# A two-layer encoder trunk on one core: a sixteenth place for expert weights, rows from 128 on stored behind the pair's rows, idle products on the matrix engine, and gathers by expert pair

## The chip, the core and the metric

One core of a Trainium2 chip runs the whole program. Five engines work side by side: PE (matrix products), DVE and ACT (elementwise work and reductions; ACT also has function tables that must be loaded), POOL, and SP, which here only issues transfers. Each runs its own instructions in order and waits on semaphores for the others. Weights come from the chip's memory through 16 DMA engines. The metric is the device time in microseconds (us) of one execution; less is better.

## The reference, cut to what matters

256 tokens of width 1024 go through two layers. Each layer has a mixer (two linear recurrences, attention over all tokens, gates) and a feed-forward part. In the first layer this part is dense (width 2816); in the second it is eight experts of width 3584, of which a router picks two for each token:

```python
def moe_swiglu(h, router_w, router_b, w_gate, w_up, w_down):
    t = h.reshape(B * S, D)
    logits = (t @ router_w).astype(jnp.float32) + router_b.astype(jnp.float32)
    top_vals, top_idx = lax.top_k(logits, TOP_K)
    top_w = jax.nn.softmax(top_vals, axis=-1)
    combine = jnp.sum(jax.nn.one_hot(top_idx, N_EXPERTS) * top_w[..., None], axis=1)
    for e in range(N_EXPERTS):
        y = swiglu(t, w_gate[e], w_up[e], w_down[e])
        out = out + combine[:, e:e + 1] * y
...
h = modulate(x, sh1, sc1); x = x + g1 * hybrid_mixer(h, ...)
h = modulate(x, sh2, sc2); x = x + g2 * ff
return rms_norm(x, final_gain)
```

Everything is float32, and the expert weights are 352 MB of the 516 MB that are read.

## The kernel before, in words

**Dense stages.** Mixer, dense feed-forward and second mixer are one list of units (34, 33 and 34 of them). A unit is a weight block of 128 x 2048 floats (1 MB). ACT rounds it to a high part, DVE or POOL makes the low part, and PE multiplies high and low parts with those of the activations, 48 products of 256 columns in a unit (L397). `Run.go` writes the units one after the other, and `run.at(u, pe, ev)` hangs other work on a unit; that written order is the order on each engine.

Three places of these stages matter here. `Norm.scale` (L344 to L351) stands between two stages: the sums of squares (L316, products with one column), the root on ACT and DVE (`root`), a diagonal matrix `dg` on DVE, and one product `rb` that spreads the row factors over all partitions; DVE then makes `h` (L375), ACT `hh` (L377), DVE `hl` (L364), and the first unit starts. `heads` (L676 on) does attention two heads at a time: scores, softmax on ACT, DVE and POOL, and `turn_pe` (L701), which transposes the probabilities on PE into banks `prT`; the first two heads of a layer have nothing before them that PE could do meanwhile. In `moe`, the router picks (DVE), five small products count each expert's tokens (`posp`, L1098 to L1102), and DVE makes positions from them.

**Experts.** The eight experts are handled in four pairs. Each pair has 84 weight blocks of 1 MB, two to a unit: 42 units in the order of the table `TOGETHER`, which alternates the pair's experts A and B. The blocks of all pairs run through a ring of `R["size"]` places, 15 here, in a fixed order: before unit i, SP may issue the blocks up to 2i + 15 of the pair (`fetch_moe`), as far as the places they go to have been read. The tokens of an expert are gathered into `xs` by products with a one-hot matrix: `pick` makes it on DVE, `gather` (L1126) does 8 products of 128 columns for each half of the width, and ACT or DVE scales the result. Expert 0 is gathered before the first branch, expert 1 inside pair 0, and those of the next pair inside a pair, at units 13, 14 and 19, 20. Rows of an expert from 128 on are gathered at the start of its own pair into another buffer, `xbig`, which holds the place of `xT`.

What a pair does depends on how many tokens its two experts got: a `Switch` (L1485) on a register jumps to one of five written-out ways or to a general one. In the execution profiled here, pairs 0 and 3 have at most 64 rows for each expert, pair 1 has 96 and 64, pair 2 has 160 and 32. After the last pair all ways join again, and the final norm and the output (L1490 to L1500) follow.

Of the kernel before, what the change touches and what calls it, by code (L numbers as in the profile page):

```python
# [38 lines left out]
def trunk(tc, a, out, dbg=None):  # L39
# [38 lines left out]
    def pd(name, shape):  # L78
        return psp.tile(shape, F32, name=name, tag="d", bufs=4)

# [217 lines left out]
    class Norm:  # L298
# [162 lines left out]
    def mixer(l, nrm, run, U):  # L461
# [210 lines left out]
        def heads(h0, u):  # L672
# [175 lines left out]
    def ffn(nrm, run, U):  # L848
# [85 lines left out]
        def pre():  # L934
            nrm.scale(pd)
            M["hh"], M["hl"] = nrm.split(0, 3, 4)
# [107 lines left out]
    def moe(nrm):  # L1044
# [9 lines left out]
        R["ring"].append(buf("big2", [128, 2048], F32, "ring2"))  # L1054
        assert len(R["ring"]) == R["size"]
# [40 lines left out]

        pp = pd("posp", [128, 3, 8])
# [14 lines left out]
        xs = [big("xs", F32, (128, 2, ND, 128)) for _ in range(2)]  # L1112
        xbig = act.tile([128, 2, ND, 128], F32, name="xbig", tag="xT", bufs=1)
# [6 lines left out]
        def pick(e, second=False):  # L1120

            oh = buf("t1k", [128, 2, 128], name="oh")
            for t in range(2):
                V.tensor_scalar(oh[:, t, :], iota, (pos2 if second else pos)[:, t, e:e + 1], None, op0=OP.is_equal)
            return oh

        def gather(oh, x, q):

            p = pm("gat", [128, 4, 128])
            for j in range(4):  # L1130
                k = 4 * q + j
                for t in range(2):
                    PE.matmul(p[:, j, :], th[:, t, k * 128:(k + 1) * 128], oh[:, t, :], start=(t == 0), stop=(t == 1))  # L1133

            def ev():
                for j in range(4):
                    k = 4 * q + j
                    w, b = modcol(1, 4, k), modcol(1, 3, k)
                    if q:
                        V.tensor_scalar(x[:, k, :], p[:, j, :], w, b, op0=OP.mult, op1=OP.add)  # L1140
                    else:
                        S.activation(x[:, k, :], p[:, j, :], AF.Identity, scale=w, bias=b)

            return ev

        def x_of(e):
            return xs[e // 2 % 2][:, e % 2]

        class Flow:
# [15 lines left out]
            def gather(self, u, e, x, second=False):  # L1165
                st = {}
                self.at(u, ev=lambda: st.update(o=pick(e, second)))
                for q in range(2):
                    self.at(u + 1 + q, lambda q=q: st.update({q: gather(st["o"], x, q)}), lambda q=q: st[q]())
# [9 lines left out]
        class Expert:  # L1179
            def __init__(self, e, q, flow):  # L1180

                self.e, self.flow = e, flow
# [4 lines left out]
            def x(self, g, k):  # L1187
                x = x_of(self.e) if g < 2 else xbig[:, self.e % 2]
                return x[:, k, g % 2 * 64:g % 2 * 64 + self.size[g]]
# [145 lines left out]

        def gate_row(flow):
# [22 lines left out]
        def together(p, qa, qb):  # L1359

            f = Flow()
            X = {"A": Expert(2 * p, qa, f), "B": Expert(2 * p + 1, qb, f)}
# [30 lines left out]
            X["B"].end()  # L1393

        def alone(e, n, base):
# [4 lines left out]
            if n > 2:  # L1400
                o = pick(e, True)
                for q in range(2):
                    gather(o, xbig[:, e % 2], q)()
# [12 lines left out]
        def general(p, doubled, groups):  # L1416

            base = PAIR * p
            if p == 0:
                f = Flow()  # L1420
                f.units = [lambda raw: None] * 10
                f.gather(0, 1, x_of(1))
                gate_row(f)
                f.go(lambda i: None)
            if p + 1 < NE // 2:
                for e in (2 * p + 2, 2 * p + 3):
                    o = pick(e)
                    for q in range(2):
                        gather(o, x_of(e), q)()
            else:  # L1430
                nc.sync.dma_start(out=fgrow, in_=a["final_gain"][None, :].partition_broadcast(128))
                S.activation(buf("sqt", [128, 1]), eps, AF.Sqrt)
# [9 lines left out]
            fetch_moe(base + PAIR + R["size"])  # L1442

# [17 lines left out]
        oh0 = pick(0)  # L1461
        evs = [gather(oh0, x_of(0), q) for q in range(2)]
# [5 lines left out]
        V.tensor_scalar(pos2, pos, -128.0, None, op0=OP.add)  # L1468
        V.tensor_scalar(pw[:, :, 0:1], pw[:, :, 1:2], 1.0, None, op0=OP.add)
# [20 lines left out]
        fr = Norm()  # L1490
        ss = buf("rs", [128, 2])
        V.tensor_tensor(out=ss, in0=fs[:, :, 0], in1=fs[:, :, 1], op=OP.add)
        fr.root(ss)
        for t in range(2):
            to = out[0, t * 128:(t + 1) * 128, :]
            S.activation(acc[:, t, 0:512], acc[:, t, 0:512], AF.Identity, scale=fr.rs[:, t:t + 1])
            nc.sync.dma_start(out=to[:, 0:512], in_=acc[:, t, 0:512])
            V.scalar_tensor_tensor(out=acc[:, t, 512:], in0=acc[:, t, 512:], scalar=fr.rs[:, t:t + 1], in1=fgrow[:, 512:],
                                   op0=OP.mult, op1=OP.mult)
            nc.sync.dma_start(out=to[:, 512:], in_=acc[:, t, 512:])  # L1500
# [179 lines left out]
```

## Time and profile before

| | us |
|---|---|
| median of 3 runs (1655.19 to 1655.99) | 1655.61 |
| the profiled execution, its own time | 1658.49 |
| its span from the first to the last instruction | 1656.6 |

| engine | busy us | share of the span |
|---|---|---|
| PE | 1514.3 | 91% |
| DVE | 662.1 | 40% |
| ACT | 502.7 | 30% |
| POOL | 54.1 | 3% |

The chain that ended last is 66% PE, 16% DMA, 11% DVE, 4% ACT and 2% "issue" (an engine that waits for nothing the profile shows). DMA moved 519 MB. Read the span in stages: the dense stages end at about 741 us, the pairs of experts begin at about 753, 954, 1195 and 1453 us, and the last products end at 1644 us.

### The profile page before, as it was taken

How to read it: one execution, taken by the hardware profiler on the slowest of the kernel's cores; microseconds unless marked ns; L12 is line 12 of the kernel's file. 1: busy time of each engine (PE TensorE's matmuls, PEld its weight loads, DVE VectorE, ACT ScalarE, POOL GpSimd, SP SyncE). 2: the span in 40 equal slices, each digit the busy share in tenths (PEclk: the TensorE clock that was granted, in tenths of full speed). 3: DMA queues.
4: the chain of work that ended last, by engine and by line, in shares of the span. 5: the costliest groups of instructions: out<-in, count | busy, mean ns of one | idle time of the engine just before them, and what ended most of it. 6: DMA issues, size and time to landing. Idle time of an engine off the chain costs nothing.

```text
span 1656.6 us, 24634 instructions
## 1 busy us (share of the span) xinstructions
PE 1514.3 (91%) x10475; PEld 988.1 (60%) x10475; DVE 662.1 (40%) x1046; ACT 502.7 (30%) x815; POOL 54.1 (3%) x86
## 2 busy tenths in 40 slices
PE   3997999999999989989998789999699999999885
PEld 3987898999999879985433233433334434433232
DVE  7679777768666797852010100110100101200002
ACT  4775644444447756431110001101011101000001
POOL 0000002000010000110000000000000000000000
PEclk9999999999999989999999989999899999999998
DMA  9736655777846457679999999999678889889995
GB/s 357 269 123 216 234 199 192 273 277 270 301 170 236 141 190 252 230 305 388 414 421 421 418 414 407 420 406 421 249 305 359 347 345 387 361 347 421 422 421 212
DMA packets 73154, 519.27 MB, mean 313 GB/s; under 512 B 8289, under 2 KB 9185, under 8 KB 10273
## 3 DMA queue, kind: packets, MB, share of 16 engines
q1 hardware_dynamic: 67104, 475.15, 72.6%
q0 software_dynamic: 5888, 42.08, 7.1%
q8 instruction: 89, 1.46, 0.4%
q14 instruction: 73, 0.59, 0.1%
HBM read 516.01 MB, written 1.05 MB: 312 GB/s over the span
## 4 chain that ended last, share of the span: by engine, by line
PE 66%; DMA 16%; DVE 11%; ACT 4%; issue 2%; SPq 0%; DVEq 0%; ACTq 0%
PE gt L397 21%; PE egu L1216 21%; PE Y L1261 11%; PE dacc L877 4%; DMA raw<-in_moe_w_down_dram 4%; PE gat L1133 2%; DMA raw<-in_moe_w_up_dram 2%; DMA wl1r<-in_moe_w_up_dram 2%; DVE raw L243 2%; DVE wl L174 1%; DMA wh0r<-in_moe_w_down_dram 1%; DMA ring<-in_moe_w_up_dram 1%; DMA wl0r<-in_moe_w_down_dram 1%; DMA wh1r<-in_moe_w_up_dram 1%; DMA raw<-in_moe_w_gate_dram 1%
## 5 line engine op out<-in xcount | busy, mean ns | idle before, releaser
L1226 DVE TENSOR_TENSOR A<-A,egu 64x512 f32<-64x512 f32 (+1 forms) x77 | 47.5, 617 | 615.9 <-ACT A L1225 615.7
L1216 PE MATMUL egu<-raw,xs 128*64 128x512 f32 (+1 forms) x1240 | 239.0, 529 | 10.7 <-DMA raw<-in_moe_w_up_dram 4.8
L168 ACT CAST wh<-raw 128x2048 fp32r<-128x2048 f32 x101 | 192.6, 1908 | 166.5 <-PE gt L397 117.0
L397 PE MATMUL gt<-hh,wh 128*128 128x256 f32 x864 | 211.9, 293 | 21.0 <-DVE qu L615 9.4
L397 PE MATMUL gt<-hl,wh 128*128 128x256 f32 x864 | 205.8, 285 | 0.0
L397 PEld LDWEIGHTS gt<-hh,wh 128*128 128x128 f32 x864 | 167.1, 199 | 24.5 <-issue 10.8
L1225 ACT ACTIVATE A<-egu 64x512 f32<-64x512 f32 (+1 forms) x77 | 41.0, 532 | 450.3 <-PE egu L1216 350.9
L1261 PE MATMUL Y<-raw,AT 128*64 128x512 f32 (+1 forms) x784 | 161.7, 513 | 6.5 <-DMA raw<-in_moe_w_down_dram 6.4
L397 PEld LDWEIGHTS gt<-hl,wh 128*128 128x128 f32 x864 | 162.8, 192 | 0.0
L174 DVE TENSOR_TENSOR wl<-raw,wh 128x2048 fp32r<-128x2048 f32 x68 | 155.4, 2286 | 17.9 <-ACT wh L168 16.6
L1216 PEld LDWEIGHTS egu<-raw,xs 128*64 128x64 f32 (+1 forms) x1240 | 79.2, 129 | 125.1 <-issue 92.9
L1216 PE MATMUL egu<-ring,xs 128*64 128x512 f32 (+1 forms) x528 | 141.2, 546 | 9.3 <-issue 5.2
L243 DVE SCALAR_TENSOR_TENSOR raw<-raw,crow 128x1024 f32<-128x1024 f32 x96 | 115.2, 1220 | 3.4 <-DMA raw<-in_w_mod_dram 3.2
L1261 PEld LDWEIGHTS Y<-raw,AT 128*64 128x64 f32 (+1 forms) x784 | 52.7, 126 | 96.2 <-issue 74.4
L397 PE MATMUL gt<-hh,wl 128*128 128x256 f32 x688 | 96.6, 296 | 5.5 <-DVE wl L174 5.5
L397 PEld LDWEIGHTS gt<-hh,wl 128*128 128x128 f32 x688 | 91.0, 200 | 6.5 <-DVE wl L174 5.9
L1216 PE MATMUL egu<-wl1r,xs 128*64 128x512 f32 (+1 forms) x256 | 89.3, 530 | 2.4 <-DMA wl1r<-in_moe_w_up_dram 2.4
L1216 PEld LDWEIGHTS egu<-ring,xs 128*64 128x64 f32 (+1 forms) x528 | 43.8, 131 | 65.6 <-issue 52.2
L1216 PE MATMUL egu<-wh1r,xs 128*64 128x512 f32 (+1 forms) x232 | 78.4, 523 | 3.8 <-DMA wh1r<-in_moe_w_up_dram 3.8
L1241 ACT COPY AT<-aT 128x256 f32<-128x256 f32 x56 | 20.2, 373 | 201.9 <-PE aT L1235 201.5
L174 DVE TENSOR_TENSOR raw<-raw,wh 128x2048 fp32r<-128x2048 f32 x31 | 70.9, 2286 | 0.7 <-ACT wh L168 0.7
L1216 PE MATMUL egu<-wh2r,xs 128*64 128x512 f32 (+1 forms) x152 | 49.6, 522 | 6.1 <-DMA raw<-in_moe_w_up_dram 6.1
(303 smaller groups left out, 2270.0 us busy)
## 6 DMA issues: line engine op xcount, KB each, us to landing
raw<-in_moe_w_down_dram SPq DMA_DIRECT2D x57, 1024.0 KB, 14.5
raw<-in_moe_w_up_dram SPq DMA_DIRECT2D x56, 1024.0 KB, 11.1
raw<-in_moe_w_gate_dram SPq DMA_DIRECT2D x47, 1024.0 KB, 13.4
raw<-in_w_mod_dram POOLq DMA_DIRECT2D x40, 1024.0 KB, 7.4
raw<-in_w_in_T_dram SPq DMA_DIRECT2D x32, 1024.0 KB, 5.1
ring<-in_moe_w_up_dram SPq DMA_DIRECT2D x23, 1024.0 KB, 13.0
ring<-in_moe_w_gate_dram SPq DMA_DIRECT2D x22, 1024.0 KB, 16.1
ring<-in_moe_w_down_dram SPq DMA_DIRECT2D x21, 1024.0 KB, 16.2
```

Of the source, the lines that this page charges most:

```text
L168: S.copy(self.hi[j][:, c], self.raw[j][:, c])
L174: eng.tensor_tensor(out=self.lo[j][:, c0:c1], in0=self.raw[j][:, c0:c1], in1=self.hi[j][:, c0:c1].bitcast(F32), op=OP.subtract)
L243: V.scalar_tensor_tensor(out=r, in0=r, scalar=1.0, in1=crow, op0=OP.mult, op1=OP.mult, accum_out=c)
L397: PE.matmul(st["p"][f][:, 0, :], w[:, k, f * 128:(f + 1) * 128], xv[:, k, :], start=(f == fs[0] and k == 0 and v == 0 and first), stop=(no ...
L877: PE.matmul(M["dac"][dt // 2][:, dt % 2, :], w[:, i * D + dt * 128:i * D + (dt + 1) * 128], M["A", b][v][:, i, :], start=(v == 0 and not s ...
L1133: PE.matmul(p[:, j, :], th[:, t, k * 128:(k + 1) * 128], oh[:, t, :], start=(t == 0), stop=(t == 1))
L1216: PE.matmul(self.E[s][g][h, :], self.x(g, k), w[m][:, kk, cc], start=(k == 0), stop=(k == ND - 1))
L1225: S.activation(A, E[0:64, :], AF.Silu)
L1226: V.tensor_tensor(out=A, in0=A, in1=E[64:128, :], op=OP.mult)
L1241: S.copy(at[:, g], p)
L1261: PE.matmul(self.Y[g][h, :], self.A[s][:, g, j, 0:self.size[g]], w[c][:, j, cc], start=(s == 0 and j == 0), stop=(s == NF - 1 and j == 3))
```

## The change

- The ring gets a sixteenth place: the buffer of `xT`, which is free once the residual has been turned into rows. `xbig` leaves it: rows from 128 on go behind the pair's rows, into the last quarter of the two `xs` buffers.
- A pair's rows are now 192 columns (128 of A, 64 of B) and are gathered together: 16 products of 192 columns, in four steps of 4. Those of pair 0 stand before the first branch; those of the next pair hang on units 13 to 16. The one-hot matrix for rows from 128 on (`oh2`) is made a pair earlier.
- `turn_over` writes idle products (256 columns, into a bank that is overwritten or not read) at four kinds of places: 5 ahead of the first transposes of a layer's attention, 4 ahead of the product `rb` and 2 behind it in the two scalings between stages, 4 ahead of the counting products.
- The final norm and the output are written inside every way of the last pair and no longer behind the join.

```diff
+    def turn_over(bank, n):
+        for _ in range(n):
+            PE.matmul(bank, ones, con[:, 0:256], start=True, stop=True)
...
-        def scale(self, bank):
+        def scale(self, bank, idle=(0, 0)):
             self.root()
+            self.rb = bank("rb", [128, T])
+            turn_over(self.rb, idle[0])
             dg = buf("t1k", [128, 2, 128], name="dg")
...
-            self.rb = bank("rb", [128, T])
             PE.matmul(self.rb, ones, dg.rearrange("p t n -> p (t n)"), start=True, stop=True)
+            if idle[1]:
+                turn_over(pm("idle", [128, T]), idle[1])
...
                     H["t", n] = pm("prT", [128, 2, T])
+                    if h0 + n == 0:
+                        turn_over(H["t", n][:, 0, :], 5)
...
-                nrm.scale(pd)
+                nrm.scale(pd, (4, 2))
...
-        R["size"] = 15
+        R["size"] = 16
...
+        R["ring"].append(act.tile([128, 2048], F32, name="ring3", tag="xT", bufs=1))
...
+        turn_over(pd("idle", [128, T]), 4)
         pp = pd("posp", [128, 3, 8])
...
-        xs = [big("xs", F32, (128, 2, ND, 128)) for _ in range(2)]
-        xbig = act.tile([128, 2, ND, 128], F32, name="xbig", tag="xT", bufs=1)
+        places = [big("xs", F32, (128, 2048)) for _ in range(2)]
+        xs = [p[:, 0:1536].rearrange("p (k s) -> p k s", k=ND) for p in places]
+        xbig = [p[:, 1536:2048].rearrange("p (k s) -> p k s", k=4) for p in places]
+        oh2 = buf("oh2", [128, 2, 128])
...
+        def pick_pair(p):
+            oh = buf("t2k", [128, 2, 192], name="oh")
+            pick_to(oh[:, :, 0:128], 2 * p)
+            pick_to(oh[:, :, 128:192], 2 * p + 1)
             return oh
         def gather(oh, x, q):
-            p = pm("gat", [128, 4, 128])
-            for j in range(4):
-                k = 4 * q + j
+            n = oh.shape[2]
+            p = pm("gat", [128, 2, n])
+            for j in range(2):
+                k = 2 * q + j
                 for t in range(2):
                     PE.matmul(p[:, j, :], th[:, t, k * 128:(k + 1) * 128], oh[:, t, :], start=(t == 0), stop=(t == 1))
...
-            def gather(self, u, e, x, second=False):
+            def gather(self, u, p):
...
-                for q in range(2):
+                for q in range(4):
...
+        def final():
+            fr = Norm()
+            ss = buf("rs", [128, 2])
...
             if p == 0:
-                f.gather(0, 1, x_of(1))
                 gate_row(f)
             if qa > 4:
-                o = pick(2 * p, True)
-                for q in range(2):
-                    gather(o, xbig[:, 0], q)()
+                gather_all(oh2, xbig)
             if p + 1 < NE // 2:
-                f.gather(12, 2 * p + 2, x_of(2 * p + 2))
-                f.gather(18, 2 * p + 3, x_of(2 * p + 3))
+                f.gather(12, p + 1)
+                f.at(18, ev=lambda: pick_to(oh2, 2 * p + 2, True))
...
             X["B"].end()
+            if p + 1 == NE // 2:
+                final()
...
-        oh0 = pick(0)
-        evs = [gather(oh0, x_of(0), q) for q in range(2)]
+        oh0 = pick_pair(0)
+        evs = [gather(oh0, xs[0], q) for q in range(4)]
```

The order of the instructions shows it at three places. On PE between the first mixer and the dense feed-forward, before (`ssq` are the sums of squares, `rb` the spread row factors, `gt` a unit's products with the high and low parts of activations and weights):

```order
L397 MATMUL gt<-mh,wl_76 128x256 x8
L316 MATMUL ssq<-ones,sq_2277 128x1 x2
L316 MATMUL ssq<-ones,sq 128x1 x4
L351 MATMUL rb<-dg,ones 128x256
L397 MATMUL gt<-hh,wh_79 128x256 x16
```

and now:

```order
L406 MATMUL gt<-mh,wl_76 128x256 x8
L322 MATMUL ssq<-ones,sq_2282 128x1 x2
L322 MATMUL ssq<-ones,sq 128x1 x4
L85 MATMUL rb<-con,ones 128x256 x4
L358 MATMUL rb<-dg,ones 128x256
L85 MATMUL idle<-con,ones 128x256 x2
L406 MATMUL gt<-hh,wh_79 128x256 x16
```

Four idle products stand between the last sum and `rb`, two between `rb` and the first unit.

On PE at the end of the router, before the first branch (`rows` turns the residual into rows, `posp` counts, `gat` gathers, `ci` is the register's source), before:

```order
L1041 MATMUL rows<-con,xT 128x128 x8
L1098 MATMUL posp<-trir 128x8
L1099 MATMUL posp<-trir 128x8
L1100 MATMUL posp<-trir 128x8
L1101 MATMUL posp<-trir 128x8
L1102 MATMUL posp<-trir 128x8
L1133 MATMUL gat<-oh,th 128x128 x16
L1463 TENSOR_LOAD ci
```

and now:

```order
L1052 MATMUL rows<-con,xT 128x128 x8
L85 MATMUL idle<-con,ones 128x256 x4
L1111 MATMUL posp<-trir 128x8
L1112 MATMUL posp<-trir 128x8
L1113 MATMUL posp<-trir 128x8
L1114 MATMUL posp<-trir 128x8
L1115 MATMUL posp<-trir 128x8
L1155 MATMUL gat<-oh,th 128x192 x16
L1502 TENSOR_LOAD ci
```

The 16 gather products are half as wide again, and four idle products stand ahead of the counts.

On ACT at the end of the last pair's way, before, with the rows behind the join of all ways after the "..." (`fsq` are the squares of the last sum, `rsy` the root):

```order
L1377 ACT_TABLE_LOAD
L1377 ACTIVATE sqt<-eps 128x1
L1332 ACTIVATE fsq,fs<-acc 128x512 x4
L1676 UNCONDITIONAL_BRANCH
...
L337 ACT_TABLE_LOAD
L337 ACTIVATE rsy<-rs,eps 128x2
L1496 ACTIVATE acc<-acc,rsy 128x512 x2
L1676 UNCONDITIONAL_BRANCH
```

and now:

```order
L1414 ACT_TABLE_LOAD
L1414 ACTIVATE sqt<-eps 128x1
L1359 ACTIVATE fsq,fs<-acc 128x512 x4
L343 ACTIVATE rsy<-rs,eps 128x2
L1370 ACTIVATE acc<-acc,rsy 128x512 x2
L1705 UNCONDITIONAL_BRANCH
```

The jump stands behind the output now, and the second load of the table is not there any more.

## Rows read from the trace of the kernel before

**Rows 1.** Chain that ended last, in order of time: start us, us, what.

```profile
956.50 19.77 DMA wh1r<-in_moe_w_gate_dram
976.40 11.81 PE egu L1216 x62
...
1605.41 19.80 DMA raw<-in_moe_w_down_dram
```

**Rows 2.** Windows of 20 us: stretch, length, busy us by engine, granted clock, DMA share, GB/s.

```profile
1240.00:1260.00 20.00, 20.00 (x220) 8.83 (x218) 0.42 (x1) 1.46 (x5) 0.00 (x0) 1.00 0.85 342
...
1480.00:1500.00 20.00, 20.00 (x100) 7.01 (x100) 1.38 (x2) 1.92 (x4) 0.00 (x0) 1.00 1.01 419
```

**Rows 3.** Windows of 2 us at five places.

```profile
194.00:196.00 2.00, 1.70 (x7) 1.30 (x8) 2.00 (x3) 1.85 (x2) 1.28 (x2) 0.50 0.11 16
...
644.00:646.00 2.00, 0.41 (x2) 0.20 (x2) 1.29 (x3) 2.00 (x6) 1.00 (x1) 1.00 0.06 25
...
740.00:742.00 2.00, 1.29 (x7) 0.89 (x5) 1.79 (x16) 1.11 (x3) 0.00 (x0) 0.50 0.98 401
...
756.00:758.00 2.00, 2.00 (x12) 0.86 (x10) 0.00 (x0) 0.00 (x0) 0.00 (x0) 1.00 0.48 86
...
1456.00:1458.00 2.00, 2.00 (x10) 0.73 (x8) 0.00 (x0) 0.00 (x0) 0.00 (x0) 0.83 0.01 4
```

**Rows 4.** Chain that ended last: first unit behind each layer's first softmax.

```profile
199.90 6.05 PE gt L397 x48
...
648.95 5.69 PE gt L397 x48
```

**Rows 5.** Timeline, first transposes of each layer: start, us, instruction, idle before and its end.

```profile
193.99 0.66 PE L706 MATMUL prT<-con,pr 128*128 128x128 f32 x2 [2.46 <-DVE pr L697]
...
645.39 0.41 PE L706 MATMUL prT<-con,pr 128*128 128x128 f32 x2 [2.26 <-DVE pr L697]
```

**Rows 6.** Timeline at the two scalings between stages.

```profile
285.66 0.61 PE L316 MATMUL ssq<-ones,sq 128*128 128x1 f32 x4 [0.24 <-ACT sq L305]
288.23 0.70 PE L351 MATMUL rb<-dg,ones 128*128 128x256 f32 x2 [1.96 <-DVE dg L348]
...
289.48 3.30 ACT L377 ACTIVATE hh<-h,modc 128x256 fp32r<-128x256 f32 x8 [2.91 <-DVE h L375]
...
296.65 1.58 PE L397 MATMUL gt<-hl,wh 128*128 128x256 f32 x12
...
481.00 2.81 PE L316 MATMUL ssq<-ones,sq 128*128 128x1 f32 x24 [0.24 <-DVE sq L907]
...
485.48 1.22 PE L351 MATMUL rb<-dg,ones 128*128 128x256 f32 x2 [1.66 <-DVE dg L348]
```

**Rows 7.** Timeline of PE before and in the first pair.

```profile
742.63 0.38 PE L1098 MATMUL posp<-trir 128*128 128x8 f32 x1 [1.34 <-DVE trir L1091]
...
746.07 5.74 PE L1133 MATMUL gat<-oh,th 128*128 128x128 f32 x32 [2.21 <-DVE oh L1124]
752.66 7.09 PE L1216 MATMUL egu<-raw,xs 128*64 128x512 f32 x32 [0.84 <-PE gat L1133]
```

**Rows 8.** Timeline of PE, one half gather inside pair 2.

```profile
1283.26 2.05 PE L1133 MATMUL gat<-oh,th 128*128 128x128 f32 x16
```

**Rows 9.** Timeline at the starts of pairs 2 and 3.

```profile
1188.01 0.48 DVE L1124 TENSOR_SCALAR oh<-con,rt 128x128 f32<-128x128 f32 x2 [10.40 <-issue]
...
1188.45 6.39 PE L1133 MATMUL gat<-oh,th 128*128 128x128 f32 x32 [12.46 <-DVE oh L1124]
...
1452.73 6.01 PE L1216 MATMUL egu<-ring,xs 128*64 128x512 f32 x17 [5.19 <-issue]
...
1458.34 0.34 SPq L986 DMA_DIRECT2D ring<-in_moe_w_up_dram  x1
```

**Rows 10.** Timeline of the final norm.

```profile
1647.96 1.28 ACT L337 ACT_TABLE_LOAD   x1 [1.68 <-issue]
...
1649.58 0.17 DVE L339 RECIPROCAL rsy<-rsy 128x2 f32<-128x2 f32 x1 [2.34 <-ACT rsy L337]
```

More of the change, by code (lines that the diff above doesn't have):

```diff
@@ L934, in pre @@
         def pre():
-            nrm.scale(pd)
+            nrm.scale(pd, (4, 2))
             M["hh"], M["hl"] = nrm.split(0, 3, 4)
@@ L1118, in moe, with pick_to @@
         g2h, g2q = g2[:, 0:512], g2[:, 512:768]
-        def pick(e, second=False):
-            oh = buf("t1k", [128, 2, 128], name="oh")
+        def pick_to(oh, e, second=False):
             for t in range(2):
-                V.tensor_scalar(oh[:, t, :], iota, (pos2 if second else pos)[:, t, e:e + 1], None, op0=OP.is_equal)
+                V.tensor_scalar(oh[:, t, :], iota[:, 0:oh.shape[2]], (pos2 if second else pos)[:, t, e:e + 1], None,
+                                op0=OP.is_equal)
+        def pick_pair(p):
+            oh = buf("t2k", [128, 2, 192], name="oh")
+            pick_to(oh[:, :, 0:128], 2 * p)
+            pick_to(oh[:, :, 128:192], 2 * p + 1)
             return oh
         def gather(oh, x, q):
-            p = pm("gat", [128, 4, 128])
-            for j in range(4):
-                k = 4 * q + j
+            n = oh.shape[2]
+            p = pm("gat", [128, 2, n])
+            for j in range(2):
+                k = 2 * q + j
                 for t in range(2):
@@ L1135, in ev, with gather_all @@
             def ev():
-                for j in range(4):
-                    k = 4 * q + j
+                for j in range(2):
+                    k = 2 * q + j
                     w, b = modcol(1, 4, k), modcol(1, 3, k)
-                    if q:
-                        V.tensor_scalar(x[:, k, :], p[:, j, :], w, b, op0=OP.mult, op1=OP.add)
+                    xk = x[k // 4][:, k % 4, :] if isinstance(x, list) else x[:, k, 0:n]
+                    if j:
+                        V.tensor_scalar(xk, p[:, j, :], w, b, op0=OP.mult, op1=OP.add)
                     else:
-                        S.activation(x[:, k, :], p[:, j, :], AF.Identity, scale=w, bias=b)
+                        S.activation(xk, p[:, j, :], AF.Identity, scale=w, bias=b)
             return ev
-        def x_of(e):
-            return xs[e // 2 % 2][:, e % 2]
+        def gather_all(oh, x):
+            for q in range(4):
+                gather(oh, x, q)()
         class Flow:
@@ L1163, in defer @@
                 self.at(self.i + d, pe, ev)
-            def gather(self, u, e, x, second=False):
+            def gather(self, u, p):
                 st = {}
-                self.at(u, ev=lambda: st.update(o=pick(e, second)))
-                for q in range(2):
-                    self.at(u + 1 + q, lambda q=q: st.update({q: gather(st["o"], x, q)}), lambda q=q: st[q]())
+                self.at(u, ev=lambda: st.update(o=pick_pair(p)))
+                for q in range(4):
+                    self.at(u + 1 + q, lambda q=q: st.update({q: gather(st["o"], xs[p % 2], q)}), lambda q=q: st[q]())
             def go(self, raw):
@@ L1179, in moe, with __init__ @@
         class Expert:
-            def __init__(self, e, q, flow):
-                self.e, self.flow = e, flow
+            def __init__(self, e, q, flow, first=0):
+                self.e, self.flow, self.first = e, flow, first
                 self.size = [64] * (q // 2) + [32] * (q % 2)
@@ L1187, in x @@
             def x(self, g, k):
-                x = x_of(self.e) if g < 2 else xbig[:, self.e % 2]
-                return x[:, k, g % 2 * 64:g % 2 * 64 + self.size[g]]
+                if g < 2:
+                    c = self.first + 64 * g
+                    return xs[self.e // 2 % 2][:, k, c:c + self.size[g]]
+                c = 64 * g - 128
+                return xbig[k // 4][:, k % 4, c:c + self.size[g]]
             def cols(self, g):
@@ L1334, in finish @@
                 G.tensor_tensor(out=acc[:, t, cc], in0=acc[:, t, cc], in1=fgrow[:, cc], op=OP.mult)
+        def final():
+            fr = Norm()
+            ss = buf("rs", [128, 2])
+            V.tensor_tensor(out=ss, in0=fs[:, :, 0], in1=fs[:, :, 1], op=OP.add)
+            fr.root(ss)
+            for t in range(2):
+                to = out[0, t * 128:(t + 1) * 128, :]
+                S.activation(acc[:, t, 0:512], acc[:, t, 0:512], AF.Identity, scale=fr.rs[:, t:t + 1])
+                nc.sync.dma_start(out=to[:, 0:512], in_=acc[:, t, 0:512])
+                V.scalar_tensor_tensor(out=acc[:, t, 512:], in0=acc[:, t, 512:], scalar=fr.rs[:, t:t + 1], in1=fgrow[:, 512:],
+                                       op0=OP.mult, op1=OP.mult)
+                nc.sync.dma_start(out=to[:, 512:], in_=acc[:, t, 512:])
         def gate_row(flow):
@@ L1399, in alone @@
             f.units = [X.unit(kind, s, b) for _, kind, s, b in ALONE]
[L1400 to L1403, printed above, removed]
+            for second in range(2 if n > 2 else 1):
+                pick_to(oh2, e, second)
+                gather_all(oh2, xbig if second else xs[e // 2 % 2])
+            if e == NE - 1:
+                nc.sync.dma_start(out=fgrow, in_=a["final_gain"][None, :].partition_broadcast(128))
+                S.activation(buf("sqt", [128, 1]), eps, AF.Sqrt)
             f.at(ALONE.index(("A", "d", NF - 3, 0)), X.backs(0))
@@ L1421, in general @@
                 f.units = [lambda raw: None] * 10
-                f.gather(0, 1, x_of(1))
                 gate_row(f)
@@ L1425, in general @@
             if p + 1 < NE // 2:
[L1426 to L1432, printed above, removed]
+                gather_all(pick_pair(p + 1), xs[(p + 1) % 2])
             alone(2 * p, (1, 2, 4)[doubled], base)
@@ L1442, in general @@
             fetch_moe(base + PAIR + R["size"])
+            if p + 1 < NE // 2:
+                pick_to(oh2, 2 * p + 2, True)
+            else:
+                final()
         pc = pp[:, 2, :].rearrange("p (e two) -> p two e", two=2)
@@ L1489, in moe @@
                     branch(general, w - NW, cnt[2 * p + 1])
[L1490 to L1500, printed above, removed]
     nc.sync.dma_start(out=crow, in_=a["c"].partition_broadcast(128))
```

3 lines of the change are left out of this document (2 added, 1 removed).

## The prediction, made before the changed kernel ran

> **What bounds the kernel now.** I read the chain that ended last first, in order of time, because the kernel is a row of stages with different limits. Up to the router it runs almost wholly through PE. Then the weights of the first pair and a half are waited for: a transfer ends that stretch at 976.3, and from 976.40 on the chain is PE [rows 1]. It stays PE through pair 2, where PE is busy all the time and DMA only 0.85 of it, and becomes DMA again in pair 3, where DMA is at 1.01 and 419 GB/s, up to a transfer that lands at 1625.2 [rows 1, 2]. A block is 1.049 MB, so it costs 2.50 us there. Second, windows of 2 us give the granted clock around each wait of PE: 0.50 in 194 to 196 and 740 to 742, 1.00 in 644 to 646 [rows 3]. So a saving counts in three ways: before the router nearly in full; in pair 1 (behind 976) and pair 2 if it is PE's; in pair 3 only if it moves the moment from which transfers run without a pause, or the tail.
>
> The profiled execution took 1658.49 us, its span is 1656.6, the median of the runs is 1655.61. I sum against the span and take the difference from the median.
>
> **Idle products before attention.** PE waits for the softmax, 2.46 us in layer 0 and 2.26 in layer 1 [rows 5]. In layer 0 the clock is then at half, in layer 1 full [rows 3]. From the first transposes to the first unit behind them it is 199.90 - 193.99 = 5.91 against 648.95 - 645.39 = 3.56, and that unit takes 6.05 against 5.69 [rows 4, 5]: 2.35 + 0.36 = 2.7 us for the clock. What does an idle product cost? `rb` is such a product, two passes, 0.70 at full and 1.22 at half clock, a pipeline's end included [rows 6]; back to back I estimate 0.43 and 0.86. Five at full clock take 2.15, which both waits hold. So layer 0 gains 2.7 and layer 1 nothing: **-2.7**; bounds -2.7 and 0, if the clock falls all the same.
>
> **Idle products in the two scalings.** Between the first mixer and the feed-forward PE's last sum ends at 286.27 and `rb` starts at 288.23 [rows 6]: four idle products (1.7) fit into 1.96, and two more fit behind. The stage ran at half clock: its third group of 16 products started at 296.65. At full clock the first 16 follow ACT's `hh`, which ends at 292.78; the next 16 take 16 x 5.69 / 48 = 1.9, so the third group starts at 294.9 instead [rows 4, 6]: **-1.7**; bounds -1.7 and +1.5 (four at half clock, 3.4, in 1.96). The second scaling differs: PE runs 24 one-column sums for 2.81 us up to 483.81, and `rb` then takes 1.22, so the clock had fallen ahead of the idle products [rows 6]. At half clock they need 3.4 in a wait of 1.66, and DVE, which is behind `rb`, bounds the start: +1.8; at full clock they gain 0.4 on `rb`. I take **+0.3**, since part of them will run at either clock.
>
> **Before the first pair.** The idle products here stand where PE waits 1.34 us [rows 7] and the clock is at half [rows 3]: 1.7 to 3.4 us, so the counts come 0.4 to 2.1 late. The gather took 5.74 for 16 products of 128 columns (32 passes); with 192 columns I put a pass at 0.18 full and 0.32 half, so 5.7 to 10.2. The first unit thus starts 0.4 to 6.5 late. It frees the first places, and there DMA had run dry: 0.48 in 756 to 758 [rows 3], about 1.3 us in all with its edges. The sixteenth block gives it 2.5 us more to wait with. The net runs from -1.3 (no pause) to +6.5 - 2.5 = +4.0; I take a start 2.5 late, so **0**. It costs in full, because pair 0 is bound by transfers. The gathers that leave the inside of pair 0 gain nothing for the same reason.
>
> **Gathers in pairs 1 and 2.** Each held four half gathers of 2.05 (16 passes of 0.128) [rows 8], 8.2 us; now 32 passes. A pass costs 0.128 if columns were free (4.1) and 0.192 in proportion (6.1); `rb`'s 256 columns at 0.23 a pass put 192 at 0.18, so 5.8. Saved: **-2.4** in each (bounds -4.1 and -2.0). The scalings on ACT and DVE have less to do than before and lie beside PE. In pair 1 it is nothing if DMA becomes the bound there.
>
> **Start of pair 2.** PE waited for DVE's one-hot matrix, 0.48 long, and DVE itself for 10.40 us of "issue" [rows 9]. The matrix is ready a pair earlier now, so PE depends on its own jump: at least 0.4 sooner. At most: PE's whole idle time was 12.46, and at pair 3 it was 5.19 [rows 9], a difference of 7.3, of which the evictions on DVE (there from 1188.0 on) let through about 5.9. I stay near the lower end, **-1.5**: all engines pass the same jump.
>
> **The sixteenth place.** At pair 3 the ring is full: DMA 0.01 in 1456 to 1458 [rows 3], and the next block is issued only after the first unit, at 1458.34 [rows 9]. From there 69 blocks came without a pause; now one of them is already in. There was room for it: DMA stood still for over 4 us, it needs 2.5. **-2.5**; bounds -2.5 and 0.
>
> **Tail.** ACT idled 1.68 behind the join and then loaded its table for 1.28, so DVE could go on at 1649.58 [rows 10]. ACT was done with the squares at 1646.28. Without jump and table, DVE's sum (0.3) and the root (0.3) let it go on at 1647.0 to 1647.3: **-2.4** (bounds -1.3, the table alone, and -2.6). The jump now stands behind the last issues and is covered by the landing of the output.
>
> Sum: -2.7 - 1.7 + 0.3 + 0 - 2.4 - 1.5 - 2.4 - 2.5 - 2.4 = -15.3. Span 1641.3, the profiled time 1643.2, the median 1655.6 - 15.3 = 1640.3. I predict **1640.5 us**; the likeliest case's own range is 1636 to 1645.
>
> **Rivals.**
>
> *The clock is not held.* [...] Then -2.7 and -1.7 go, the second scaling costs 1.8, and the start of the pairs some 2.0: -15.3 + 4.4 + 1.5 + 2.0 = -7.4, 1648. Against it: in layer 1 the clock survived a wait of 2.26 with nothing in it [rows 3, 5]. The Trainium skill (TensorE: Matmul & The Clock Gate, Part 1) says that the monitor behind the clock runs free of the kernel's start, so in another run the clock may fall at another of these waits. By that rule the 2.7 of layer 0 might be no loss in the timed runs, and the sum would be -12.6; the two layers, with the same wait and different clocks, agree with it.
>
> *Place and gathers buy less.* If the added block isn't in before pair 3's first unit, and pair 1 stays bound by transfers, -2.5 and -2.4 go: 1645.2. For it: DMA is at 1.0 through pair 1 as well. Against it: the 4 us of standstill, and that PE, not DMA, ends the chain from 976 on.
>
> *A better jump.* If PE starts pair 2 by 5.9 earlier and transfers never pause in pair 0, 4.4 + 1.3 more: 1634.6.
>
> *Slower: code waits behind weights.* The code of a way is fetched at the jump through the same DMA engines. If the larger ring makes a fetch wait as long as a weight block issued in the crowd, 19.80 us [rows 1], PE's idle of 12.46 and 5.19 at pairs 2 and 3 grows by 7.3 + 14.6 = 21.9, and the time is 1655.6 - 15.3 + 21.9 = 1662. It decides from 15.3 us for both together. Against it: at pair 3 weights were in flight, and the idle was 5.19 only. The Trainium skill (Runtime: NRT & Kernel Launch, Instruction fetch mechanics) says that a taken branch to code that isn't held must wait for a DMA fetch; the "issue" of 10.40 agrees, and the rule holds for every new layout of code, so either jump can change in either direction.
>
> *It doesn't do what it says:* the sixteenth place could stay empty because `xT` is still read. The order puts the last reader, `rows`, ahead of the router's products, so no.
>
> **How the numbers follow.** Forecast 0.53, clock not held 0.20, place and gathers less 0.15, better jump 0.07, slower 0.03, something else that leaves no change 0.02. The range for 8 in 10 goes from 1635 to 1648. About 0.2% (3.3 us) is what a measurement of this kernel can tell from no change. Only the slower case and the edges of the first two rivals end above 1652: faster 0.92, same 0.05, slower 0.03.
>
> **What would show it.** Right: clock 1.0 through both layers' first transposes and through the start of the feed-forward; `rb` of the second scaling up to 1.8 later behind its sums; one block more issued by SP before the pairs, and no pause, or a shorter one, of DMA in the first units; gathers of 8 passes at about 1.45 us; pair 2's gather on PE without a wait for DVE; a single table load ahead of the last root. Wrong: the first unit of pair 0 over 4 us late with DMA paused as long, "issue" over 12 us at a pair's start, or waits for transfers in pair 1 behind its first units.

## The result, and the profile after

| | before | after |
|---|---|---|
| median us (4 runs each, side by side) | 1655.8 | 1628.09 |
| range us | 1655.19 to 1658.15 | 1626.96 to 1629.89 |
| ratio of the times, 95% interval | | 0.9831 (0.9814 to 0.9848) |
| span of the profiled execution, us | 1656.6 | 1625.2 |
| mean granted clock over the profiled span | 0.972 | 0.984 |

The change is worth 27.7 us by the medians and 31.4 between the two profiled spans: the profiled run of before (1658.49) was 2.7 over its median, that of after (1626.96) the fastest of its four, 1.1 under, so the stages below add up to 3.7 more than the medians. One run of the kernel before, of 8443.91 us, is left out. The forecast was 15.3, 1640.5 us, and its range (1635 to 1648) misses. The way to find what it missed is to read the same instruction in both traces, stage by stage, and to write down by how much it comes earlier. The rows of before are in the groups named; those with an asterisk were not among them.

| at | before | after | earlier by | gained in this stage | forecast |
|---|---|---|---|---|---|
| last sum of scaling 1 [rows 6] | 285.66 | 282.29 | 3.4 | 3.4, of it 0.6 ahead of any edit | 2.7 |
| third group of 16 products behind it [rows 6] | 296.65 | 291.72 | 4.9 | 1.6 | 1.7 |
| first count of the router [rows 7] | 742.63 | 737.13 | 5.5 | 0.6 | -0.3 |
| first unit of pair 0 [rows 7] | 752.66 | 748.81 | 3.9 | -1.7 | -2.5 |
| first unit of pair 1* | 953.92 | 946.26 | 7.7 | 3.8 | 2.5 |
| a unit behind pair 1's first five* | 988.60 | 973.11 | 15.5 | **7.8** | 0 |
| end of pair 1's last products* | 1175.99 | 1158.26 | 17.7 | 2.2 | 2.4 |
| gather at the start of pair 2 [rows 9] | 1188.45 | 1164.30 | 24.2 | **6.4** | 1.5 |
| first unit of pair 3 [rows 9] | 1452.73 | 1425.52 | 27.2 | 3.1 | 2.4 |
| last landing [rows 1] | 1625.2 | 1595.0 | 30.2 | 3.0 | 2.5 |
| end | 1656.6 | 1625.2 | 31.4 | 1.2 | 2.4 |

Two places hold 14 of the 31 us, and the forecast had nothing in the one and the low end in the other.

**Where the idle products stand, PE is busy and the clock is full.** PE's timeline of after at the two scalings and at layer 0's first transposes:

```profile
190.71 2.32 PE L85 MATMUL prT<-con,ones 128*128 128x256 f32 x10
193.25 0.44 PE L717 MATMUL prT<-con,pr 128*128 128x128 f32 x2 [0.21 <-DVE pr L706]
...
282.76 1.97 PE L85 MATMUL rb<-con,ones 128*128 128x256 f32 x8
284.86 0.70 PE L358 MATMUL rb<-dg,ones 128*128 128x256 f32 x2
...
291.72 2.06 PE L406 MATMUL gt<-hl,wh 128*128 128x256 f32 x16
...
480.55 0.69 PE L358 MATMUL rb<-dg,ones 128*128 128x256 f32 x2
```

The wait for the softmax is 0.21 instead of 2.46 [rows 5], ten passes take 2.32 (0.23 each, as the forecast put them), and `rb` of the second scaling takes 0.69 instead of 1.22 [rows 6]. Windows of 2 us of after (stretch, length, busy us by engine, granted clock, DMA share, GB/s) at the places of [rows 3]:

```profile
194.00:196.00 2.00, 1.71 (x11) 1.60 (x12) 1.97 (x5) 1.84 (x3) 0.96 (x3) 1.00 0.44 61
644.00:646.00 2.00, 2.00 (x19) 2.00 (x18) 1.70 (x4) 0.15 (x1) 0.00 (x0) 1.00 0.91 307
740.00:742.00 2.00, 1.58 (x5) 1.61 (x6) 0.44 (x3) 1.79 (x4) 0.00 (x0) 0.50 1.00 422
752.00:754.00 2.00, 2.00 (x12) 0.59 (x10) 0.00 (x0) 0.00 (x0) 0.00 (x0) 1.00 0.74 193
```

Before, at the second scaling, the clock was full until the sums ended at 483.81 [rows 6], and `rb` behind the wait ran at half:

```profile
482.00:484.00 2.00, 1.81 (x17) 1.73 (x16) 0.00 (x0) 0.55 (x2) 0.00 (x0) 0.97 1.00 418
```

In after, ahead of pair 0, the clock is at half: behind the counts PE waits 2.57 us more with nothing in it. DMA still pauses at the first unit, for less (0.74 in the worst window, 0.48 before).

**Before pair 0.** PE's timeline of after:

```profile
737.13 0.27 PE L1111 MATMUL posp<-trir 128*128 128x8 f32 x1 [0.23 <-DVE trir L1103]
...
740.42 8.46 PE L1155 MATMUL gat<-oh,th 128*128 128x192 f32 x32 [2.57 <-ACT pw L1118]
```

The counts are not late at all (the four products fit into the wait at full clock), and the gather takes 8.46 where the forecast had 5.7 to 10.2.

**Start of pair 1.** The chain that ended last, in order of time, of after:

```profile
901.51 19.82 DMA ring<-in_moe_w_down_dram
921.37 3.65 PE Y L1288 x14
...
946.26 17.07 PE egu L1243 x112
...
973.11 5.45 PE egu L1243 x48
```

From 921.37 on, up to pair 3, no transfer is in it. Before, the chain reaches the unit that starts at 973.11 here only at 988.60. PE's timeline of before has a stop inside pair 1, and SP's shows what was issued when:

```profile
953.92 1.08 PE L1216 MATMUL egu<-wh2r,xs 128*64 128x512 f32 x1 [6.14 <-DMA raw<-in_moe_w_up_dram]
...
971.09 1.07 PE L1216 MATMUL egu<-raw,xs 128*64 128x512 f32 x2
976.40 9.10 PE L1216 MATMUL egu<-raw,xs 128*64 128x512 f32 x28 [4.25 <-DMA wh1r<-in_moe_w_gate_dram]
```

```profile
936.65 0.33 SPq L986 DMA_DIRECT2D raw<-in_moe_w_gate_dram  x1
939.13 0.33 SPq L986 DMA_DIRECT2D raw<-in_moe_w_up_dram  x1
...
956.50 0.33 SPq L986 DMA_DIRECT2D wh1r<-in_moe_w_gate_dram  x1
```

PE stops after the first product of a unit (two passes), and what ends the stop is the landing of a block in `wh1r`. But the unit reads `raw` only: the two blocks issued at 936.65 and 939.13, which a landing 19.8 us later puts at 956.5 and 958.9, 12 us ahead of the stop's start. So this was not a wait for the weights in use. The clock fell as well (windows of before):

```profile
972.00:976.00 4.00, 0.16 (x1) 0.00 (x0) 0.00 (x0) 0.00 (x0) 0.00 (x0) 0.93 1.01 420
976.00:980.00 4.00, 3.60 (x10) 1.27 (x12) 0.00 (x0) 0.00 (x0) 0.00 (x0) 0.50 1.01 420
```

Together, with what the slower products cost, 7.8 us. What PE waited for stands in the program as built. The blocks signal their landing on eight semaphores in turn. In the way of pair 1 that ran, the first products with either of the unit's two blocks wait so (before; `raw4` and `raw5` are its two places, blocks 7 and 8 of the pair):

```
PE L1216 Matmult egu<-raw4,xs      DMA semaphore 7 >= 448
PE L1216 EventSemaphore            DMA semaphore 7 >= 464
PE L1216 Matmult egu<-raw5,xs      DMA semaphore 0 >= 480
```

Block 8 signals on semaphore 0 in the five written ways of pair 0, and on semaphore 7 in the general way. Behind the join the kernel can't know which way ran, so the reader waits for both; and on semaphore 7 the count 464 is reached by the fifteenth block, `wh1r`. That second wait stands behind the first product, where PE stopped. The ways differ because the general way loads all 84 blocks of the pair anew and then 15, the others 84 in all: 15 is no multiple of eight. With 16 places it is 16, the turn comes out the same in all ways, and after has no such second wait. That is a theory made from the program; the runs below test it.

**Start of pair 2.** PE's and DVE's timeline of after:

```profile
1164.30 6.44 PE L1155 MATMUL gat<-oh,th 128*128 128x128 f32 x32 [6.05 <-issue]
...
1170.19 1.49 DVE L1163 TENSOR_SCALAR xs<-gat,modc 128x128 f32<-128x128 f32 x4 [10.31 <-issue]
```

PE passes the jump in 6.05 and waits for nobody, DVE needs 10.31 as it did before (10.40, [rows 9]). The evictions on DVE come late now, but the gather runs almost to its end without them.

**Gathers, pair 3, tail.** The chain and the timeline of after:

```profile
1255.39 1.50 PE gat L1155 x8
...
1575.18 19.79 DMA wl1r<-in_moe_w_down_dram
1595.02 3.65 PE Y L1288 x14
```

```profile
1616.86 0.30 ACT L343 ACTIVATE rsy<-rs,eps 128x2 f32<-128x2 f32 x1 [0.79 <-DVE rs L1366]
...
1620.27 0.41 SPq L1374 DMA_DIRECT2D out_dram<-acc  x1
```

A quarter gather takes 1.50, four of them 6.0 instead of 4 x 2.05 [rows 8]. Of the 3.1 gained up to pair 3's first unit, 0.6 are not theirs: PE passes the jump into pair 3 in 4.55, before in 5.19 [rows 9]:

```profile
1425.52 3.43 PE L1243 MATMUL egu<-ring,xs 128*64 128x512 f32 x8 [4.55 <-issue]
```

From pair 3's first unit to the last landing it is 169.5 instead of 172.5. The root comes 21.8 behind the last landing instead of 24.0, but from the last issue to the end it is now 4.5 us (before: the last issue ends at 1652.98, 3.6).

### The profile page after: what moved, and what is told of

Read it like the earlier page. It is cut to its first block, busy times and chain, and to the rows that moved or that the text cites. A ratio compares the mean times of both kernels' runs of the same rounds, so it can differ in the third digit from the quotient of the medians.

```text
span 1625.2 us, 24445 instructions
## 1 busy us (share of the span) xinstructions
PE 1505.5 (93%) x10399; PEld 980.2 (60%) x10399; DVE 659.8 (41%) x1036; ACT 497.5 (31%) x798; POOL 53.7 (3%) x86
## 4 chain that ended last, share of the span: by engine, by line
PE 40%; DMA 12%; DVE 1%; issue 1%; ACT 0%; DVEq 0%; SPq 0%
PE egu L1243 23%; PE Y L1288 12%; DMA ring<-in_moe_w_up_dram 2%; DMA wl1r<-in_moe_w_up_dram 2%; PE gat L1155 2%; DMA wh0r<-in_moe_w_up_dram 1%; DMA raw<-in_moe_w_down_dram 1%; DMA wh0r<-in_moe_w_down_dram 1%; DMA ring<-in_moe_w_down_dram 1%; DMA raw<-in_moe_w_up_dram 1%; DMA wl1r<-in_moe_w_down_dram 1%; PE aT L1262 1%; PE sct L1336 1%; DVE acc L1343 1%; ACT fsq L1359 0%
## 5 line engine op out<-in xcount | busy, mean ns | idle before, releaser
L1288 PE MATMUL Y<-raw,AT 128*64 128x512 f32 (+1 forms) x760 | 138.5, 506 | 5.3 <-DMA raw<-in_moe_w_down_dram 5.3
L1243 PE MATMUL egu<-ring,xs 128*64 128x512 f32 (+1 forms) x832 | 129.4, 502 | 7.5 <-issue 4.5
L1288 PEld LDWEIGHTS Y<-raw,AT 128*64 128x64 f32 (+1 forms) x760 | 46.0, 125 | 84.2 <-issue 67.3
L1288 PE MATMUL Y<-ring,AT 128*64 128x512 f32 (+1 forms) x352 | 63.9, 519 | 5.3 <-DMA ring<-in_moe_w_down_dram 5.3
L1243 PE MATMUL egu<-wl1r,xs 128*64 128x512 f32 (+1 forms) x200 | 63.7, 511 | 2.6 <-DMA wl1r<-in_moe_w_up_dram 2.6
L1243 PE MATMUL egu<-wl0r,xs 128*64 128x512 f32 (+1 forms) x200 | 64.1, 512 | 0.0
## 6 DMA issues: line engine op xcount, KB each, us to landing
raw<-in_moe_w_down_dram SPq DMA_DIRECT2D x49, 1024.0 KB, 19.8
raw<-in_moe_w_up_dram SPq DMA_DIRECT2D x42, 1024.0 KB, 19.8
ring<-in_moe_w_down_dram SPq DMA_DIRECT2D x28, 1024.0 KB, 19.8
ring<-in_moe_w_gate_dram SPq DMA_DIRECT2D x28, 1024.0 KB, 19.8
ring<-in_moe_w_up_dram SPq DMA_DIRECT2D x28, 1024.0 KB, 19.8
```

The costliest lines, as they stand in the source:

```text
L1243: PE.matmul(self.E[s][g][h, :], self.x(g, k), w[m][:, kk, cc], start=(k == 0), stop=(k == ND - 1))
L1288: PE.matmul(self.Y[g][h, :], self.A[s][:, g, j, 0:self.size[g]], w[c][:, j, cc], start=(s == 0 and j == 0), stop=(s == NF - 1 and j == 3))
```

## The experiments

Every run stands beside runs of the kernel before on the same chip; as the medians of that kernel went from 1655.8 to 1659.2 from chip to chip, ratios are compared, and differences in us are the ratio times 1656.

**One more load in a way that does not run (before).**

```diff
             R["n"] = base + PAIR
+            if p + 1 < NE // 2:
+                for _ in range(1):
+                    nc.sync.dma_start(out=ring(R["n"]), in_=in_order(R["n"]))
             fetch_moe(base + PAIR + R["size"])
```

> The kernel before, with one more load (of the next pair's first block, twice) in the general way, which does not run here. Theory A: the eight semaphores that the loads take in turn fall out of step between the general way (84 + 15 loads) and the five written ways (84 loads), so PE's fourth unit of pair 1 also waits for the last block of the fifteen (issued 956.50, landed 976.30); 100 loads bring them into step and the wait of 4.25 us and the half clock behind it go: 1655.6 - 8 = 1648 us, PE never idle between 954 and 1010. Rival B: the wait was for weights that the unit does read, or the time came from the place or the code of the changed kernel: 1655.6, no change.

Measured: 0.9964 (0.9951 to 0.9977), 6.0 us less. The second wait is gone from the built program, and PE's timeline shows the unit without a stop:

```profile
970.24 6.23 PE L1216 MATMUL egu<-raw,xs 128*64 128x512 f32 x28
```

Theory A holds (6.0 where it said 8). Only waits differ: the way that ran has the same work as before.

**15 places in the changed kernel, without and with that load.** The first takes the sixteenth place away (`R["size"] = 15`, no `ring3`), the second adds the load above.

> The changed kernel with the ring at 15 places and everything else as it is. Theory A: the place is worth 2.5 at the end of the transfer-bound pair 0 and 2.5 again in pair 3, and the wait of pair 1 comes back for 8: 1628.1 + 13 = 1641 us, PE idle for some 4 us within pair 1's first four units. Rival B: only the place counts, 2.5 to 5: 1631 to 1633. The forecast as it was written gave the place 2.5 in pair 3 and 2.5 before pair 0.

> The changed kernel with 15 places, and one more load in the general way, which does not run here. Theory A: the ways are in step again, so the wait of pair 1 does not come; what is left is the place itself, 1628.1 + 2.5 + 2.5 = 1633 us. Rival B (the edit of a way that does not run changes nothing): the time of the 15 places without the edit.

Measured: 0.9904 (0.9888 to 0.9919) and 0.9862 (0.9846 to 0.9879). Against the changed kernel (0.9831 and, run again, 0.9828) the first loses 12 us, the second 5; the load alone is worth 7. PE's timeline of the first has the stop back; its SP's timeline has the load that ends it:

```profile
950.87 0.33 SPq L997 DMA_DIRECT2D wh1r<-in_moe_w_gate_dram  x1
...
965.78 1.07 PE L1242 MATMUL egu<-raw,xs 128*64 128x512 f32 x2
970.78 1.97 PE L1242 MATMUL egu<-raw,xs 128*64 128x512 f32 x4 [3.93 <-DMA wh2r<-in_moe_w_up_dram]
```

Here the profile names `wh2r`; its fifteenth block is again the one in `wh1r`, issued at 950.87, and 19.8 us later is 970.7. In the second the chain runs from the jump to PE without a transfer, as after:

```profile
945.96 4.66 issue
950.62 16.75 PE egu L1242 x112
...
1601.94 3.65 PE Y L1287 x14
```

So the place itself is worth 5 by the times (some 1 to 9 by the two intervals), as theory A had it. In the profiles it is 2.4 at pair 1's start (950.62 - 946.26, less the 2.0 by which pair 0 began later) and 2.2 in pair 3 (171.7 instead of 169.5 from its first unit, 1430.20, to the last landing, 1601.94).

**Out of step on purpose (after).** The same edit with `range(7)`.

> The changed kernel with 16 places, and seven more loads in the general way, which does not run here. Theory A: the ways are one semaphore out of step, so the fifth unit of pair 1 also waits for the last of the sixteen blocks (issued at 951.2, landing about 971.0) where it now starts at 966.8: 4.2 us, and 1 to 3 more for a clock that falls: 1628.1 + 4 to 7 = 1632 to 1635. Rival B: no change, 1628.1.

Measured: 0.9856 (0.9841 to 0.9871), 4 us more than after. The size is as expected, the place is not: it is pair 1's first unit that waits, 11.35 us instead of 6.26, for `wl1r`, which it does not read. PE's timeline in after and here, and the chain here:

```profile
946.26 8.61 PE L1243 MATMUL egu<-raw,xs 128*64 128x512 f32 x49 [6.26 <-issue]
...
951.85 1.98 PE L1243 MATMUL egu<-raw,xs 128*64 128x512 f32 x4 [11.35 <-DMA wl1r<-in_moe_w_up_dram]
```

```profile
931.85 19.75 DMA wl1r<-in_moe_w_up_dram
951.85 17.15 PE egu L1243 x112
```

In the general way the first block now signals on the semaphore that here carries the eighth (`wl1r`); I had looked for the last one only. The mechanism is the same, and by then the fifth unit's own wait was over.

**The early one-hot matrix alone (before).**

```diff
+                f.at(22, ev=lambda: pick_to(oh2, 2 * p + 2, True))
...
-                o = pick(2 * p, True)
                 for q in range(2):
-                    gather(o, xbig[:, 0], q)()
+                    gather(oh2, xbig[:, 0], q)()
```

> The kernel before, with the one-hot matrix for rows from 128 on made by DVE inside the pair ahead, as the changed kernel does; all else as before. Theory A: DVE's jump is the late one at pair 2 and PE waits for DVE alone, so PE's idle time there goes from 12.46 to about 6 and the time falls by 6.4. Rival B: all engines pass the same jump and PE's own is the limit, as the forecast chose: 0.4 to 1.5 less.

Measured: 0.9958 (0.9944 to 0.9973), 7 us less. PE's and DVE's timeline at pair 2:

```profile
1178.35 2.05 PE L1138 MATMUL gat<-oh,th 128*128 128x128 f32 x8 [5.67 <-issue]
...
1183.85 1.37 DVE L1145 TENSOR_SCALAR xbig<-gat,modc 128x128 f32<-128x128 f32 x4 [9.93 <-PE gat L1138]
```

PE's 12.46 became 5.67. Theory A holds: PE had waited for DVE's matrix, not for its own jump. How long DVE itself takes over the jump can't be read here, since its 9.93 us end with the gather's second half on PE (at 1183.74), which DVE's first instruction behind the jump reads.

**Idle products: out of the changed kernel, into the one before.** (`turn_over` returns at once; and the four calls of the change in the kernel before.)

> The changed kernel once more, beside the three that follow, as the measure for their small differences (the kernel before took 2.4 us more on the chip of the last four runs than on that of the first). Both theories: 0.983 of the kernel before.

> The changed kernel without any idle product. Theory A: they are worth what stands in the traces up to the router, 2.7 + 1.6 + 0.6 us, and nothing or some tenths there, 4.9 to 5.1 over the changed kernel. Rival B: the clock falls as often without them, or what is gained ahead of the transfers of pair 0 is lost there: 0 to 2.

> The kernel before with the idle products alone, at the same four kinds of places. Theory A, from the runs of the changed kernel with and without them: the granted clock of a run goes from about 0.972 to 0.982, the spread of the runs shrinks, and the median falls by 5 to 9. Rival B, the forecast's terms: 2.7 + 1.7 - 0.3 less, and up to 2 given back ahead of pair 0: 2 to 4.

Measured: after again 0.9828 (0.9812 to 0.9844); without idle products 0.9889 (0.9870 to 0.9907), 10 us more, which is more than either expectation; before with them 0.9972 (0.9963 to 0.9981), 4.6 us less, between the two expectations. The mean granted clock tells the two kinds apart: 0.979 to 0.983 in the twelve runs of before with idle products, 0.970 to 0.976 in the 22 runs of before beside them. The intervals of the two answers, some 6 to 14 and 3 to 6, hardly meet; whether idle products are worth more in the changed kernel stays open. One profile can't give the value: in the profiled run without them the clock is full at layer 0's softmax and at half at layer 1's, the other way round than in [rows 3], and both were without idle products.

```profile
194.00:196.00 2.00, 2.00 (x13) 1.79 (x12) 1.97 (x4) 0.80 (x2) 0.53 (x1) 1.00 0.84 225
642.00:644.00 2.00, 1.57 (x7) 1.57 (x8) 1.97 (x5) 1.59 (x2) 0.95 (x3) 0.50 0.41 61
```

The rule of the Trainium skill that the forecast cited (TensorE: Matmul & The Clock Gate, Part 1), that the monitor behind the clock runs free of the kernel's start, agrees with that.

**Five more idle products behind the counts (after).**

> The changed kernel with five more idle products between the counting products and pair 0's gather, where PE waits 2.57 us for DVE. Theory A: the gather runs at full clock, 5.8 instead of 8.46, and pair 0's first unit starts 2 to 2.6 earlier; but transfers bound pair 0 and pause 0.76 us only, so the time falls by no more than 0.8. Rival B: what PE gains goes through, 2 to 2.6.

Measured: 0.9823 (0.9809 to 0.9837), beside 0.9828 of the changed kernel: no difference that the times can tell, and neither expectation is excluded by them. PE's timeline ahead of pair 0 and at pair 1:

```profile
741.68 5.44 PE L1156 MATMUL gat<-oh,th 128*128 128x192 f32 x32 [0.30 <-ACT pw L1119]
747.05 2.37 PE L1244 MATMUL egu<-raw,xs 128*64 128x512 f32 x10
...
946.91 1.98 PE L1244 MATMUL egu<-raw,xs 128*64 128x512 f32 x4 [4.79 <-DMA ring<-in_moe_w_gate_dram]
```

The gather takes 5.44, pair 0 begins 1.5 us sooner than in the changed kernel run beside it (748.54), and pair 1 at the same time (946.84 there). By the traces it is A: what PE gains ahead of pair 0 doesn't reach pair 1. This version is no better than the change.

**The final norm inside the ways alone (before).**

> The kernel before, with the final norm and the output written inside every way of the last pair instead of behind the join; all else as before. Theory A, from the changed kernel's trace: the root comes 2.2 us sooner after the last transfer, but about 1 us of it is given back behind the output, where the jump now stands: from the last landing to the end 31.35 becomes 30.2, and the time falls by 1.2, which the times alone can hardly show. Rival B, the forecast: the landing of the output covers the jump, so 2.4 less, 29.0 from the last landing to the end.

Measured: 0.9990 (0.9977 to 1.0002): the time alone tells nothing. The trace does: the last transfer lands at 1625.2, the span ends at 1655.3, 30.1 instead of 31.35, as in A. SP's last issue:

```profile
1650.51 0.41 SPq L1347 DMA_DIRECT2D out_dram<-acc  x1
```

From its end to the end of the span it is 4.4 us, before 3.6. Of the 2.2 that the root gains nearly half is given back, most of it behind the output, where the edit put the jump.

**Do the parts add up?** Four edits together on the kernel before, and beside it the changed kernel with 15 places and one more load, which has the gathers by pair besides.

> The kernel before with the four edits that were tried alone on it, together: one more load in the general way, the early one-hot matrix, the idle products, the final norm inside the ways; still 15 places and a gather for each expert. Theory A (they add up): -6.0 - 7.0 - 4.6 - 1.2 to -1.6 = -19, 0.9885 of the kernel before. Rival B (a part of one is paid for by another, since idle products and the wait of pair 1 both sit ahead of the same transfers): -12 to -15.

> The changed kernel with 15 places and one more load in the general way, once more, beside the one above, from which it then differs by the gathers by expert pair alone. Theory A: the gathers buy what the traces show, 2.2 in pair 1 and up to 3.1 in pair 2, so this kernel is 4 to 5.5 faster than the one above. Rival B: pair 1's part is lost to the transfers, 2 to 3.

Measured: 0.9887 (0.9864 to 0.9910), where A had 0.9885; the interval, 15 to 22.5 us, leaves of B only its upper end. One of these five runs took 1642.17 us at a mean clock of 0.955, the others 1635.54 to 1637.70 at 0.980 to 0.985: the idle products are in that run too, and where its clock fell is not shown. The second kernel: 0.9859 (0.9838 to 0.9880), 4.6 less. The intervals overlap, so the gathers are shown by the traces (1.50 against 2.05) and only agreed with by the times. The parts, by ratio: the wait 6 to 7, the early matrix 7, idle products 4.6, the gathers 4.6, the place 5, the tail 1.2 (by the trace), together 28.4 to 29.4, where 27.7 were measured at first and 28.5 the second time. The sum takes idle products at 4.6; with the 10 of the changed kernel it would be some 34, so that it comes out is no proof of each part. The place is the least sure one: this repeat of the 15 places has 5 by ratio again, but its profile, beside that of the changed kernel run again, gives 1.5 in pair 0 (199.8 instead of 198.3 us from its first unit to pair 1's) and 1.1 in pair 3 (172.0 instead of 170.9 from its first unit to the last landing).

## Why the prediction was wrong

The direction and most of the mechanisms were right; two steps failed, each because of how a row was read: a wait in pair 1 that the sum had no term for, and the size of the term for the start of pair 2.

- **What bounds the kernel now, first paragraph.** "The weights of the first pair and a half are waited for: a transfer ends that stretch at 976.3" [rows 1]. The row was read as a wait for data. It was a wait for a semaphore that some other way might have used, and the change removed it: 6 to 7 us (the first three experiments), 7.8 in the profiles. The names were there to see: the released products read `raw`, the releaser wrote `wh1r`. The forecast then took pair 1 as bound by transfers up to 976 and had no term for it.
- **Start of pair 2, -1.5.** It had both ends, 0.4 and 5.9, and took the low one because "all engines pass the same jump". They pass it at different speeds: DVE 10.40 and 10.31 (before and after), PE 6.05 and 5.67 (after, and before with the early matrix). The row that showed it was there: PE's idle time at pair 3, 5.19, where it waits for no DVE [rows 9]. The part is worth 6.4 to 7, so the upper end was too low as well: the cap for evictions on DVE did not bind, as PE had run 5.9 of the gather's 6.44 us when DVE's first eviction began (1170.19).
- **Heads -2.7, scaling 1 -1.7**: 2.7 and 1.6 in the profiles. **Scaling 2 +0.3**: 0.6 gained; the idle products ran at full clock there. The reading "the clock had fallen ahead of the idle products" was wrong: by the window shown above it fell at the end of the sums, just where the products now begin. The value over many runs may be more than the one pair of traces gave (4.6, and some 10 in the changed kernel); that the clock falls at other waits in other runs is seen in one profile, and whether it makes up the rest is not shown. The rival "the clock is not held" is refuted by the windows at the two layers' attention and by `rb` at both scalings; ahead of pair 0 the clock did fall, behind the counts.
- **Before the first pair, 0.** The start came 1.7 late instead of 2.5, the block and the shorter pause gave 3.8: a gain of 2.1, outside the range of that term (-1.3). Of the 3.8, 2.4 are the block's by the run with 15 places and one more load; the other 1.4 were not tried alone.
- **Gathers -2.4 each**: 2.2, and 3.1 less the 0.6 of the shorter jump. **The sixteenth place -2.5 in pair 3**: 3.0 in the profile, 2.2 and 1.1 by the two runs with 15 places. Both right within that scatter.
- **Tail -2.4**: 1.2. The step that failed is "the jump now stands behind the last issues and is covered by the landing of the output": from the last issue to the end it is 4.4 to 4.5 us instead of 3.6.
- **The rivals.** "A better jump" came true, with the pause not quite gone. "Place and gathers buy less" did not: both terms came. "Code waits behind weights" did not: PE's "issue" at pairs 2 and 3 was 6.05 and 4.55.

The range was too narrow because it was built from the terms alone. No term stood for a wait of before that the edit removes without meaning to, although the ring's size stands in every way's order of loads.

## What to carry to other kernels

In the row of a wait compare the tile that ended it with the tiles that the waiting instruction reads: if they differ, the wait may be one of bookkeeping, which can be removed without making anything faster. It is not proof: ahead of pair 1's first unit the profile of before also names a transfer that the unit doesn't read (6.14 us), and that of after, for the same jump and 6.26 us, nobody. The waits in the program as built decide. Where written ways join and semaphores are used in turn, give every way the same count of issues modulo the number of semaphores, the ways that never run too. At a jump look at each engine's own "issue" time, and give the first instruction behind it nothing that the slowest engine has still to make.

## What had not been expected of the hardware

The engines take unlike times over one jump: into pair 2 DVE idles 9.03 to 11.13 us (the six traces that name nobody it waited for), PE 4.4 to 6.3 wherever it waits for no other engine behind the jump. And the time of one kernel spreads from run to run by more than most parts of this change: before took 1653.69 us in a run at a mean clock of 0.976 and 1659.59 in one at 0.970. The clock tells only a part of it, since another run took 1661.01 at 0.973.
